# A hybrid decoder layer on one core: ten quads of seven products instead of nine in eleven column pairs, bias loaded for four heads at once

## The chip, the cores and the metric

The kernel runs on one core of one Trainium2 chip. The metric is the device time of one execution in microseconds. All values are float32 in and out. The core's engines are TensorE (PE in the profile, with PEld for the loading of weights), VectorE (DVE), ScalarE (ACT), GpSimd (POOL) and SyncE (SP), which only issues transfers here.

## The reference

One layer: an RMS norm, one input projection to eight parts of 2048 columns, block-sparse attention with a bias by relative position on four of them, a short causal convolution on the other four, an output projection and a second RMS norm. The sequence has 256 positions, the width is 4096, there are 16 heads of 128, and with a block of 256 every query sees only its own block, so the attention is plain causal attention.

```
u = rmsnorm(x, norm_gain)                      # x: 256 x 4096
proj = u @ w_in                                # 4096 x 16384
q, k, v, z_a, hc, b_gate, c_gate, z_c = split(proj, 8)
l = q @ k.T * 128**-0.5 + bias[bucket(qpos - kpos)], causal     # per head
attn = softmax(l) @ v * silu(z_a)
conv = b_gate * short_conv(c_gate * hc, conv_w) * silu(z_c)     # three taps
h = x + concat(attn, conv) @ w_out             # 4096 x 4096
out = rmsnorm(h, final_gain)
```

Nearly all of the work is the two products with w_in (256 MB) and w_out (64 MB), which are read once.

## The kernel before

**Products.** The weights are taken in 20 pairs of column blocks of 512 (16 pairs of w_in, 4 of w_out). Within a pair the 4096 rows are taken as 16 quads: a quad is two row blocks of 128 times two column blocks of 512, one transfer of 1 MB. With the two halves of the 256 positions, a quad is a 2 x 2 times 2 x 2 block product. It is made in one of two ways: with eight block products, or with seven (Winograd's form of Strassen's algorithm). `ORDERS` gives the order of a pair's quads and `SEVENS` those of them that are made with seven; both come from a pattern string, in which S stands for a quad of seven and P for one of eight. Here a capital S or the word seven means such a quad. Products are summed over the quads in eight PSUM banks.

**Precision.** Each float32 operand is split into a rounded high part and the rest (hi and lo, lines 592 and 594), and each block product is three matmuls of 128 x 128 by 128 x 512: high by high, low by high, high by low (lines 666, 667 and 669). The cast to hi runs on ACT, the difference lo on DVE. An S needs, beside the split of the four raw blocks, three sums of blocks (lines 574 and 575 on DVE) and their split. A first sum of two blocks is made in DRAM ahead of time by a copy (SP, line 509) and an accumulating transfer (POOL, line 510), for at most three quads ahead.

**Units and rings.** A P is one unit of eight products, an S two units: four products with the raw blocks, then three with the sums. `split(u + 2)` loads, sums and splits two units ahead of PE; hi and lo have three slots each, the raw blocks three tiles. The stationary operands, made from x or from the mixer's output, stay in SBUF for all pairs (tiles k0 to k15): four parts for a quad that is always P, seven or eight where it is ever S (`SIZES`). The eighth is needed where a quad is S in one pair and P in a later one, because an S needs a difference in place of part 0 (`g_at`, `BOTH`). `made_up` makes the additional parts of a quad between two pairs (`RAISE`).

**Closing of a pair.** The last S of a pair finishes four banks, which `early` takes out (line 376 on ACT, lines 377 to 379 on DVE). The other four are taken behind the last quad by `two_done` (line 389). The last two quads of every pair are P.

**Attention and convolution** are laid between the products by counts of products: `tasks_of(p)` counts from the last S of pair p, `heads_of(p)` from the opening of the pair. The scores of the four heads of a group (`turn`, `scores`) run in the last two quads of pairs 1, 3, 5 and 7, the probabilities (`probs`) there and in the first quad of the next pair, `values` and `mixed` at the end of pairs 2, 4, 6 and 8; the convolutions at the end of pairs 10, 12, 14 and in pair 16. `bias_load` loads the bias of one head with eight transfers from a DRAM table, called in `scores` for the head after the next one (lines 262 to 272, 290), so that behind each addition (line 289) eight transfers stand in SP's queue. The pools' planner (the tile framework) places the instructions of each engine's queue by their readiness under its own costs, with the order of the program as priority; so neighbours in a queue can change places.

Of the kernel before, what the change touches and what calls it, by code (L numbers as in the profile page):

```python
# [10 lines left out]
F32 = mybir.dt.float32  # L11
# [6 lines left out]
P = 128  # L18
# [21 lines left out]
        "9": "PSPSSPSSPSSPSSPP", "m": "PSPSSPSPSSPSPSSP", "e": "PSPSPSPSPSPSSPPP", "f": "PSPSSPSPSSPSSPPP"}  # L40
KIND = "01999999" "99999999" "099e"
# [23 lines left out]
SEVEN = (0, 2, 4, 6, 8, 10, 12, 14, 11)  # L65
# [17 lines left out]
def of(pattern):  # L83
    n = pattern.count("S")
    return in_order(pattern, SEVEN[:n], EIGHT + SEVEN[n:]), set(SEVEN[:n])
# [7 lines left out]
BOTH = {q for q in range(NQ) for a, b in ((0, N_PAIRS), (N_PAIRS, N_PAIRS + NDP)) for p in range(a, b)  # L93
        if q in SEVENS[p] and any(q not in SEVENS[x] for x in range(p, b))}
# [5 lines left out]
RAISE = {(1, 1): 4, (1, 3): 6, (1, 6): 0, (1, 8): 2, (1, 10): 11,  # L100
# [8 lines left out]
def hymba_layer(ctx: ExitStack, tc: tile.TileContext, xT, xres, gain, w, convw, wout,  # L109
# [61 lines left out]
    def x_load(q):  # L171
        xr = pool.tile([P, 2, S], F32, name="xr", tag="pt", bufs=4)
        nc.sync.dma_start(xr, xT[q].rearrange("p (k t) -> p k t", k=2))
        return xr

# [40 lines left out]
    def squares(n):  # L216
        p, t = divmod(n, 2)
        xq = pool.tile([P, 2, B], F32, name="xq", tag="qk"[t]).rearrange("p n c -> p (n c)")
        nc.sync.dma_start(xq, xres[p][:, t * 2 * B:(t + 1) * 2 * B])
        nc.scalar.activation(xq, xq, AF.Square, accum_out=sx[:, t, p:p + 1])  # L220
# [22 lines left out]
    def bias_rows():  # L243

        tab = pool.tile([BUCKETS + 1, H], F32, name="tab", tag="lg", bufs=2)
        nc.vector.memset(tab, MASKED)
        nc.sync.dma_start(tab[:BUCKETS], relb)
        oh = pool.tile([BUCKETS + 1, 384], F32, name="oh", tag="bt", bufs=2)
# [3 lines left out]
        row = pool.tile([H, 384], F32, name="row", tag="lg", bufs=2)  # L252
# [9 lines left out]
    def bias_load(h):  # L262
        if h >= H:
            return
        bt = BT[h] = pool.tile([P, 384], F32, name="bt", bufs=2)

        base = bias_d.offset + h * COPIES * 384
        for a in range(0, P, COPIES):
            for c0, c1, at in ((0, S, P - 1), (S, 384, S - 1)):
                nc.sync.dma_start(bt[a:a + COPIES, c0:c1],  # L270
                                  bass.AP(tensor=bias_d.tensor, offset=base + at - a,
                                          ap=[[383, COPIES], [1, c1 - c0]]))
# [10 lines left out]
    def scores(h, n):  # L283
        qk, bt = QK.pop(h), BT.pop(h)
        ps = bank(n)
        nc.tensor.matmul(ps[:, :S], qk[:, P:S], qk[:, S:], start=True, stop=True)  # L286
        nc.tensor.matmul(ps[:, S:384], qk[:, :P], qk[:, S:384], start=True, stop=True)
        lg = pool.tile([P, 384], F32, name="lg", bufs=2)
        nc.vector.tensor_tensor(lg, ps[:, :384], bt, ALU.add)
        bias_load(h + 2)  # L290
        st = pool.tile([P, 6], F32, name="st", bufs=5)
        for i, (a, b) in enumerate(((0, S), (S, 384))):
            nc.vector.tensor_reduce(st[:, i:i + 1], lg[:, a:b], axis=AX.X, op=ALU.max, negate=True)
            nc.scalar.activation(lg[:, a:b], lg[:, a:b], AF.Exp, bias=st[:, i:i + 1],  # L294
                                 accum_out=st[:, 2 + i:3 + i])
        nc.vector.reciprocal(st[:, 4:6], st[:, 2:4])
        SM[h] = lg, st

    def probs(h, n):
        ps = bank(n)  # L300
        lg, st = SM[h]
        for j in range(3):
            nc.tensor.transpose(ps[:, j * P:(j + 1) * P], lg[:, j * P:(j + 1) * P], ident)  # L303
        PT[h] = pool.tile([P, 2 * S], F32, name="pt", bufs=4)[:, :384]
        nc.scalar.copy(PT[h], ps[:, :384])
# [206 lines left out]
    def load(n):  # L512
# [5 lines left out]
        if p == 0:  # L518
            if i == 0:
                nc.scalar.dma_start(g_sb, gain)  # L520
                xr = xrs[q] = pool.tile([P, 2, S], F32, name="xr", tag="pt", bufs=4)
                nc.scalar.dma_start(xr[:, 1], xT[q][:, S:])
            else:
                xrs[q] = x_load(q)
# [147 lines left out]
    for u, (n, kind, at, products) in enumerate(units):  # L672
# [36 lines left out]
        if p == 1 and i in (0, 4, 5):  # L709
            if i:  # L710
                bias_load(i - 4)
            else:
                bias_store(row)
# [22 lines left out]
        if (p, i + 1) in RAISE:  # L736
            q = RAISE[p, i + 1]
            raised[q] = x_load(q) if p < N_PAIRS else m_load(q)
        if (p, i) in RAISE:
            q = RAISE[p, i]  # L740
            made_up(q, x_scaled(q, raised.pop(q)) if p < N_PAIRS else raised.pop(q))
# [87 lines left out]
```

## Time and profile before

| what | value |
|---|---|
| time, median of 3 runs | 1698.26 us (1697.95 to 1698.77) |
| span of the profiled execution | 1696.2 us |
| PE, DVE, ACT busy | 99%, 90%, 62% of the span |
| granted TensorE clock | 0.998 |
| matmuls of the products | three lines, 2370 records each under their main operands |
| transfers | 452 MB, mean 267 GB/s |

The profile gives one execution, whose own time is the span of 1696.2 us from the first to the last instruction; the timed runs include what lies around it. Records are named by line, engine and operation and by the tiles out<-in. A matmul's record overlaps that of the next one. "Idle before" is an engine's idle time ahead of an instruction, with what ended it.

### The profile page before, as it was taken

Reading aid. Unit: us, or ns where it says so; the run is one execution under the profiler, and the core shown is the slowest. Engines: PE = TensorE matmul, PEld = TensorE weight load, DVE = VectorE, ACT = ScalarE, POOL = GpSimd, SP = SyncE. Lnnn points to the kernel's source line nnn. Section 1 sums busy time; section 2 is a strip of 40 time slices with the busy share of each in tenths; the row PEclk is TensorE's granted clock in tenths of the full one; section 3 lists DMA queues with packets and bytes.
Section 4 is the critical chain, followed back from the end, with each engine's and each line's share of the span. In section 5 each row is a group of like instructions: output and inputs, shape, how many; then the busy total and the mean of one; then the engine's idle time right before and its main releaser. Section 6 shows DMA issues by size and latency. Waiting matters only on the chain.

```text
span 1696.2 us, 20730 instructions
## 1 busy us (share of the span) xinstructions
PE 1682.2 (99%) x7562; PEld 1388.8 (82%) x7562; DVE 1527.7 (90%) x1307; ACT 1056.1 (62%) x1167; POOL 128.8 (8%) x162
## 2 busy tenths in 40 slices
PE   9999999999999999999999999999999999999997
PEld 7888888888888888888888888888888888878886
DVE  7989889888988898898998989899999999989887
ACT  6856755675667565755566565656565755656553
POOL 0000000000000000000000000000001000101000
PEclk9999999999999999999999999999999999999999
DMA  8878878778887878787888888888888889989884
GB/s 337 292 243 281 241 249 283 265 240 260 267 261 244 276 246 276 235 264 257 263 274 268 269 265 278 270 252 272 272 273 258 293 281 300 286 267 268 293 281 168
DMA packets 116625, 452.36 MB, mean 267 GB/s; under 512 B 16459, under 2 KB 21356, under 8 KB 93292
## 3 DMA queue, kind: packets, MB, share of 16 engines
q1 hardware_dynamic: 93772, 409.99, 67.2%
q0 software_dynamic: 22464, 40.90, 15.3%
q8 instruction: 59, 0.97, 0.2%
q14 instruction: 42, 0.34, 0.1%
q10 hardware_dynamic: 288, 0.15, 0.0%
HBM read 441.81 MB, written 90.96 MB: 314 GB/s over the span
## 4 chain that ended last, share of the span: by engine, by line
PE 98%; ACT 1%; issue 0%; DMA 0%; DVE 0%; DVEq 0%; SPq 0%; ACTq 0%
PE p L666 32%; PE p L667 32%; PE p L669 32%; PE p L279 0%; PE p L303 0%; ACT hi L592 0%; PE p L286 0%; DMA xr<-in_xT_dram 0%; ACT L294 0%; ACT L399 0%; PE p L312 0%; PE p L314 0%; PE p L313 0%; PE p L338 0%; PE p L358 0%
## 5 line engine op out<-in xcount | busy, mean ns | idle before, releaser
L666 PE MATMUL p<-hi,k 128*128 128x512 f32 x2370 | 921.8, 390 | 1.4 <-ACT hi L592 0.9
L667 PE MATMUL p<-hi,k 128*128 128x512 f32 x2370 | 922.5, 390 | 0.0
L592 ACT CAST hi<-raw 128x1024 fp32r<-128x1024 f32 (+1 forms) x638 | 636.5, 1044 | 302.5 <-PE p L667 224.2
L594 DVE TENSOR_TENSOR lo<-raw,hi 128x2048 fp32r<-128x2048 f32 (+1 forms) x323 | 723.5, 2247 | 70.6 <-ACT hi L592 70.3
L669 PE MATMUL p<-lo,k 128*128 128x512 f32 x2370 | 637.3, 392 | 0.0
L666 PEld LDWEIGHTS p<-hi,k 128*128 128x128 f32 x2370 | 445.0, 188 | 94.9 <-ACT hi L592 1.3
L667 PEld LDWEIGHTS p<-hi,k 128*128 128x128 f32 x2370 | 444.8, 188 | 93.3 <-issue 0.6
L669 PEld LDWEIGHTS p<-lo,k 128*128 128x128 f32 x2370 | 442.6, 188 | 89.1 <-DVE lo L594 0.3
L592 ACT CAST hi<-sum 128x1536 fp32r<-128x1536 f32 x156 | 231.2, 1482 | 207.6 <-DVE sum L575 111.5
L594 DVE TENSOR_TENSOR lo<-sum,hi 128x1536 fp32r<-128x1536 f32 x156 | 273.5, 1753 | 28.2 <-ACT hi L592 26.6
L510 POOL DMA_DIRECT2D t<-in_w_dram x126 | 103.6, 822 | 1205.4 <-DMA t<-in_w_dram 958.0
L575 DVE TENSOR_TENSOR sum<-raw,sum 128x1024 f32<-128x1024 f32 x156 | 190.7, 1222 | 3.3
L574 DVE TENSOR_TENSOR sum<-raw 128x512 f32<-128x512 f32 x156 | 106.9, 685 | 9.0 <-DMA raw<-in_w_dram 8.3
L385 ACT ACTIVATE es<-es,rT 128x512 f32<-128x512 f32 x56 | 38.9, 719 | 15.5 <-DVE es L379 8.6
L510 POOL DMA_DIRECT2D t<-in_wout_dram x30 | 24.6, 820 | 298.4 <-DMA t<-in_wout_dram 259.6
L377 DVE TENSOR_TENSOR es<-p,es 128x512 f32<-128x512 f32 x20 | 13.8, 690 | 25.9 <-PE p L669 23.8
L592 ACT CAST hi<-hg 128x1536 fp32r<-128x1536 f32 x10 | 14.8, 1480 | 24.2 <-DVE hg L575 19.6
L376 ACT COPY es<-p 128x512 f32<-128x512 f32 x20 | 11.7, 583 | 26.8 <-PE p L669 26.8
L168 ACT CAST k<-c 128x512 fp32r<-128x512 f32 (+4 forms) x38 | 21.7, 598 | 8.0 <-DVE c L165 4.8
L169 DVE TENSOR_TENSOR k<-c,k 128x512 fp32r<-128x512 f32 (+4 forms) x38 | 24.3, 661 | 2.4 <-ACT k L168 2.4
L379 DVE TENSOR_TENSOR es<-p,es 128x1024 f32<-128x1024 f32 x20 | 24.4, 1218 | 0.1
L165 DVE TENSOR_TENSOR c<-c 128x128 f32<-128x128 f32 x72 | 17.7, 285 | 0.1
(112 smaller groups left out, 528.3 us busy)
## 6 DMA issues: line engine op xcount, KB each, us to landing
raw<-in_w_dram SPq DMA_DIRECT2D x128, 1024.0 KB, 6.3
raw<-in_w_dram SPq DMA_DIRECT2D x126, 768.0 KB, 6.2
raw<-t SPq DMA_DIRECT2D x156, 256.0 KB, 4.2
raw<-in_wout_dram SPq DMA_DIRECT2D x34, 1024.0 KB, 6.5
t<-in_w_dram SPq DMA_DIRECT2D x126, 256.0 KB, 6.3
t<-in_w_dram POOLq DMA_DIRECT2D x126, 256.0 KB, 5.9
raw<-in_wout_dram SPq DMA_DIRECT2D x30, 768.0 KB, 6.7
t<-in_wout_dram SPq DMA_DIRECT2D x30, 256.0 KB, 6.8
```

Of the source, the lines that this page charges most:

```text
L168: nc.scalar.copy(dst[:, :, 0], c)
L169: nc.vector.tensor_tensor(dst[:, :, 1], c, dst[:, :, 0].bitcast(F32), ALU.subtract)
L379: nc.vector.tensor_tensor(es[:, 1::2], acc[5][:, None, :].to_broadcast([P, 2, B]), es[:, 1:3], ALU.subtract)
L385: nc.scalar.activation(e, e, AF.Copy, scale=r)
L510: nc.gpsimd.dma_start(by_rows(t1), rest[:, :B], accum_op=ALU.add)
L574: nc.vector.tensor_tensor(t[:, 0], raw[:, 0], raw[:, 2], ALU.subtract)
L575: nc.vector.tensor_tensor(t[:, 1:], raw[:, 1::2], t[:, :1].to_broadcast([P, 2, B]), ALU.subtract)
L592: nc.scalar.copy(hi[:, b:b + half], src[:, b:b + half])
L594: nc.vector.tensor_tensor(lo[:, c], src[:, c], hi[:, c].bitcast(F32), ALU.subtract)
L666: nc.tensor.matmul(acc[b_], a, h_, start=s0, stop=False)
L667: nc.tensor.matmul(acc[b_], b, h_, start=False, stop=False)
L669: nc.tensor.matmul(acc[b_], a, l_, start=False, stop=s1)
```

## The change

Pairs 2 to 10, 12 and 14 take a new pattern t with ten S in place of nine: quad 9 is made with seven there. Pairs 11, 13, 15, 17 and 18 keep nine. Because quad 9 is S in some pairs and P in later ones, its operand tile has eight parts, and pair 1 makes the extra four behind its thirteenth quad. To make room in SBUF, the operands of quads 14 and 11 in the output pairs get seven parts instead of eight, and pair 19, where both are P, makes part 0 again from DRAM (`BACK`); the bias of a group of four heads is one tile, loaded by eight transfers at places 4 to 11 of pairs 1, 2, 4 and 6, and the logits are made in place in it; tiles of x, of the squares and of the bias table take the space of others (tags q, k, es, pt). A raised x quad is loaded right into the tile in which it is scaled. The reciprocals of the sums of exponentials move from `scores` to `probs`.

```
-KIND = "01999999" "99999999" "099e"
+        "t": "PSSPSSSPSSPSSSPP"}
+KIND = "01tttttt" "ttt9t9t9" "099e"
...
-SEVEN = (0, 2, 4, 6, 8, 10, 12, 14, 11)
+SEVEN = (0, 2, 4, 6, 8, 10, 12, 14, 11, 9)
...
+BOTH = {q for q in range(NQ) for p in range(N_PAIRS)
+        if q in SEVENS[p] and any(q not in SEVENS[x] for x in range(p, N_PAIRS))}
+LAST = N_PAIRS + NDP - 1
+BACK = dict(zip(((LAST, 2), (LAST, 6)), (q for q in ORDERS[LAST] if q in SEVENS[LAST - 1] - SEVENS[LAST] - BOTH)))
...
-RAISE = {(1, 1): 4, (1, 3): 6, (1, 6): 0, (1, 8): 2, (1, 10): 11,
+RAISE = {(1, 1): 4, (1, 3): 6, (1, 6): 0, (1, 8): 2, (1, 10): 11, (1, 12): 9,
...
+    def x_again(q):
+        c = ep.tile([P, 8, P], F32, name="c", bufs=2)
+        nc.sync.dma_start(c[:, :4], xT[q].rearrange("p (a b) -> p a b", a=4))
+        return c
+
+    def scale_again(q, c):
+        for j in range(2):
+            x = c[:, 2 * j:2 * j + 2]
+            nc.scalar.activation(x, x, AF.Copy, scale=g_sb[:, 2 * q + j:2 * q + j + 1])
+        return c
...
+    def bias_load(g, n):
+        if n == 0:
+            BT[g] = pool.tile([P, HG, 384], F32, name="bt")
+        a, (c0, c1, at) = n // 2 * COPIES, ((0, S, P - 1), (S, 384, S - 1))[n % 2]
+        nc.sync.dma_start(BT[g][a:a + COPIES, :, c0:c1],
+                          bass.AP(tensor=bias_d.tensor,
+                                  offset=bias_d.offset + g * HG * COPIES * 384 + at - a,
+                                  ap=[[383, COPIES], [COPIES * 384, HG], [1, c1 - c0]]))
...
-        lg = pool.tile([P, 384], F32, name="lg", bufs=2)
-        nc.vector.tensor_tensor(lg, ps[:, :384], bt, ALU.add)
-        bias_load(h + 2)
+        nc.vector.tensor_tensor(lg, ps[:, :384], lg, ALU.add)
...
-        nc.vector.reciprocal(st[:, 4:6], st[:, 2:4])
         SM[h] = lg, st
...
     def probs(h, n):
         ps = bank(n)
         lg, st = SM[h]
+        nc.vector.reciprocal(st[:, 4:6], st[:, 2:4])
...
+        if p in (1, 2, 4, 6) and 4 <= i < 12:
+            bias_load(p // 2, i - 4)
...
+        if (p, i + 1) in BACK:
+            raised[BACK[p, i + 1]] = m_load(BACK[p, i + 1])
+        if (p, i) in BACK:
+            parts(A[BACK[p, i]][:, :1], raised.pop(BACK[p, i])[:, :1])
```

More of the change, by code (lines that the diff above doesn't have):

```diff
@@ L83, in of @@
 def of(pattern):
-    n = pattern.count("S")
-    return in_order(pattern, SEVEN[:n], EIGHT + SEVEN[n:]), set(SEVEN[:n])
+    seven = SEVEN[:pattern.count("S")]
+    eight = dict.fromkeys(EIGHT + SEVEN[len(seven):])
+    return in_order(pattern, seven, [q for q in eight if q not in seven]), set(seven)
 ORDERS, SEVENS = zip(*([(FIRST0, {8, 10, 12, 14}), (SECOND, {4, 6, 8, 10, 12, 14})]
@@ L91 @@
                        + [(FIRST, {8, 6, 10, 12, 14})] + [of(PATS[k]) for k in KIND[N_PAIRS + 1:]]))
-BOTH = {q for q in range(NQ) for a, b in ((0, N_PAIRS), (N_PAIRS, N_PAIRS + NDP)) for p in range(a, b)
-        if q in SEVENS[p] and any(q not in SEVENS[x] for x in range(p, b))}
+BOTH = {q for q in range(NQ) for p in range(N_PAIRS)
+        if q in SEVENS[p] and any(q not in SEVENS[x] for x in range(p, N_PAIRS))}
+LAST = N_PAIRS + NDP - 1
+BACK = dict(zip(((LAST, 2), (LAST, 6)), (q for q in ORDERS[LAST] if q in SEVENS[LAST - 1] - SEVENS[LAST] - BOTH)))
+assert set(BACK.values()) | BOTH >= {q for p in range(N_PAIRS, LAST) for q in SEVENS[p] - SEVENS[LAST]}
+assert all(q in SEVENS[x] for q in BACK.values() for x in range(N_PAIRS + 1, LAST))
 SIZES = [8 if q in BOTH else 7 if any(q in x for x in SEVENS) else 4 for q in range(NQ)]
@@ L169, in parts, with x_tile, x_load @@
         nc.vector.tensor_tensor(dst[:, :, 1], c, dst[:, :, 0].bitcast(F32), ALU.subtract)
-    def x_load(q):
-        xr = pool.tile([P, 2, S], F32, name="xr", tag="pt", bufs=4)
+    def x_tile(i):
+        if i % 2 == 0:
+            cur["xr"] = pool.tile([P, 2, 2, S], F32, name="xr", tag="qk"[i // 2 % 2])
+        return cur["xr"][:, i % 2]
+    def x_load(i, q):
+        xr = x_tile(i)
         nc.sync.dma_start(xr, xT[q].rearrange("p (k t) -> p k t", k=2))
         return xr
+    def x_again(q):
[7 more added lines that the diff above has]
+        return c
     def x_scaled(q, xr):
@@ L217, in squares @@
         p, t = divmod(n, 2)
-        xq = pool.tile([P, 2, B], F32, name="xq", tag="qk"[t]).rearrange("p n c -> p (n c)")
+        if n == 0:
+            cur["xq"] = ep.tile([P, 4, B], F32, name="es")
+        xq = cur["xq"][:, 2 * t:2 * t + 2].rearrange("p n c -> p (n c)")
         nc.sync.dma_start(xq, xres[p][:, t * 2 * B:(t + 1) * 2 * B])
@@ L243, in bias_rows @@
     def bias_rows():
[L245 removed]
+        tab = pool.tile([BUCKETS + 1, H], F32, name="tab", tag="pt", bufs=4)
         nc.vector.memset(tab, MASKED)
         nc.sync.dma_start(tab[:BUCKETS], relb)
[L248 removed]
+        oh = pool.tile([BUCKETS + 1, 384], F32, name="oh", tag="pt", bufs=4)
         nc.sync.dma_start(oh, onehot)
@@ L251, in bias_rows @@
         nc.tensor.matmul(ps[:H, :384], tab, oh, start=True, stop=True)
-        row = pool.tile([H, 384], F32, name="row", tag="lg", bufs=2)
+        row = pool.tile([H, 384], F32, name="row", tag="pt", bufs=4)
         nc.vector.tensor_copy(row, ps[:H, :384])
@@ L260, in hymba_layer @@
     V, Z, Q, K, QK, SM, PT, AM, BT, MT = [{} for _ in range(10)]
[L262 to L272, printed above, removed]
+    def bias_load(g, n):
+        if n == 0:
+            BT[g] = pool.tile([P, HG, 384], F32, name="bt")
[4 more added lines that the diff above has]
+                                  ap=[[383, COPIES], [COPIES * 384, HG], [1, c1 - c0]]))
     def turn(h, n):
@@ L301, in probs @@
         lg, st = SM[h]
+        nc.vector.reciprocal(st[:, 4:6], st[:, 2:4])
         for j in range(3):
             nc.tensor.transpose(ps[:, j * P:(j + 1) * P], lg[:, j * P:(j + 1) * P], ident)
-        PT[h] = pool.tile([P, 2 * S], F32, name="pt", bufs=4)[:, :384]
+        PT[h] = pool.tile([P, 384], F32, name="pt", bufs=4)
         nc.scalar.copy(PT[h], ps[:, :384])
@@ L520, in load @@
                 nc.scalar.dma_start(g_sb, gain)
-                xr = xrs[q] = pool.tile([P, 2, S], F32, name="xr", tag="pt", bufs=4)
+                xr = xrs[q] = x_tile(i)
                 nc.scalar.dma_start(xr[:, 1], xT[q][:, S:])
             else:
-                xrs[q] = x_load(q)
+                xrs[q] = x_load(i, q)
         if n < LEAD:
@@ L708, in hymba_layer @@
                 token_scale()
[L709 to L713, printed above, removed]
+        if (p, i) == (1, 0):
+            bias_store(row)
+        if p in (1, 2, 4, 6) and 4 <= i < 12:
+            bias_load(p // 2, i - 4)
         if i == last_seven[p]:
```

8 lines of the change are left out of this document (4 added, 4 removed).

## The prediction, made before the change was run

> **What bounds the kernel now.** I read the first and fifth parts of the page first: who is busy, and with what.
>
> ```profile
> span 1696.2 us, 20730 instructions
> PE 1682.2 (99%) x7562; PEld 1388.8 (82%) x7562; DVE 1527.7 (90%) x1307; ACT 1056.1 (62%) x1167; POOL 128.8 (8%) x162
> ...
> L666 PE MATMUL p<-hi,k 128*128 128x512 f32 x2370 | 921.8, 390 | 1.4 <-ACT hi L592 0.9
> ...
> L592 ACT CAST hi<-sum 128x1536 fp32r<-128x1536 f32 x156 | 231.2, 1482 | 207.6 <-DVE sum L575 111.5
> L594 DVE TENSOR_TENSOR lo<-sum,hi 128x1536 fp32r<-128x1536 f32 x156 | 273.5, 1753 | 28.2 <-ACT hi L592 26.6
> ...
> L575 DVE TENSOR_TENSOR sum<-raw,sum 128x1024 f32<-128x1024 f32 x156 | 190.7, 1222 | 3.3
> L574 DVE TENSOR_TENSOR sum<-raw 128x512 f32<-128x512 f32 x156 | 106.9, 685 | 9.0 <-DMA raw<-in_w_dram 8.3
> ```
>
> TensorE (PE) is busy for 99% of the span and waits 1.4 us in all at its main line. But a matmul record lasts 390 ns and overlaps the next, so busy time does not give the pace. The chain of waits does. Here it is at the opening of pair 10, where each row of eight closes one quad of eight products:
>
> ```profile
> 860.99 1.81 PE p L669 x8
> 866.43 1.81 PE p L669 x8
> 876.63 1.81 PE p L669 x8
> 891.59 1.81 PE p L669 x8
> ```
>
> Two eights in a row lie 5.44 us apart: 24 matmuls of 0.227 us. From 866.43 to 876.63 there is one seven and one eight, 10.20 us, so a seven takes 4.76. From 876.63 to 891.59 two sevens and an eight take 14.96 = 5.44 + 2 x 4.76. PE runs at one pace without holes, and **a quad that goes from eight products to seven saves 0.68 us** (three matmuls), if PE stays the bound.
>
> Whether it does is a question for VectorE (DVE). The view of busy time by stretches answers it, cut where ScalarE (ACT) takes the first finished sum of a pair (line 376), so that a stretch holds the last two quads of one pair and the first fourteen of the next. Columns: stretch, its length, then PE, PEld, DVE, ACT and POOL busy, the granted clock, the share of the DMA engines, GB/s.
>
> ```profile
> 79.30:161.80 82.50, 82.50 (x364) 68.04 (x363) 74.91 (x89) 53.60 (x69) 2.62 (x3) 1.00 0.77 252
> 161.80:249.70 87.90, 87.90 (x406) 72.87 (x405) 77.10 (x67) 58.16 (x72) 7.41 (x9) 1.00 0.85 263
> 249.70:333.60 83.90, 83.90 (x388) 69.57 (x387) 75.45 (x59) 51.31 (x53) 7.37 (x9) 1.00 0.81 261
> ...
> 764.80:850.00 85.20, 85.20 (x393) 70.80 (x393) 76.32 (x60) 50.66 (x52) 7.38 (x9) 1.00 0.84 259
> 850.00:930.90 80.90, 80.90 (x359) 66.98 (x358) 73.59 (x52) 50.66 (x50) 7.39 (x9) 1.00 0.85 275
> 930.90:1013.70 82.80, 82.80 (x374) 68.55 (x373) 77.64 (x64) 49.87 (x51) 7.38 (x9) 1.00 0.85 264
> ...
> 1258.40:1340.80 82.40, 82.40 (x373) 68.22 (x372) 80.12 (x73) 52.52 (x57) 7.38 (x9) 1.00 0.84 267
> ...
> 1432.30:1507.20 74.90, 74.90 (x332) 62.00 (x331) 71.55 (x53) 42.67 (x42) 7.38 (x9) 1.00 0.90 282
> 1507.20:1589.50 82.30, 81.43 (x359) 66.87 (x359) 76.23 (x54) 49.23 (x50) 7.39 (x9) 1.00 0.84 269
> 1589.50:1666.30 76.80, 76.80 (x340) 63.62 (x339) 68.13 (x49) 46.34 (x46) 3.28 (x4) 1.00 0.76 267
> ```
>
> PE fills every stretch here but the one from 1507.20 on. DVE has 10.8 us free in pair 2's stretch (161.80), 8.45 in pair 3's, 8.9 in pair 9's and 7.3 in pair 10's (850.00). Pair 15's stretch is the measure of how far this can go: DVE 80.12 of 82.40, 97.2%, and PE still full. What DVE's free time consists of:
>
> ```profile
> DVE lo L594 <- ACT hi L592: 96.9, 119, 4.0
> DVE es L377 <- PE p L669: 23.8, 10, 4.3
> DVE sum L574 <- DMA raw<-in_w_dram: 8.3, 8, 1.9
> DVE st L296 <- ACT lg L294: 7.5, 8, 1.2
> ...
> ACT hi L592 <- PE p L667: 307.6, 241, 5.1
> ```
>
> Most of it is the wait for a cast, and the cast waits for PE to give back a slot of the three-deep ring (last row): DVE waits because it is ahead, so this time can be used.
>
> **The change part by part.** The pattern t has ten S (sevens) where 9 has nine, in pairs 2 to 10, 12 and 14: eleven quads lose three matmuls each. PE: 11 x 0.68 = **7.48 us less**.
>
> *DVE.* An eight needs one L594 of 128x2048; a seven needs that one too, and 0.685 + 1.222 + 1.753 = 3.66 us more. A t stretch is 0.68 shorter as well, so DVE's free time falls by 4.34: to 6.5 in pair 2's stretch, 4.1 in pair 3's, 4.6 in pair 9's and 3.0 in pair 10's, the tightest of those quoted: 77.25 of 80.22, 96.3%, still under the 97.2% of pair 15. The conv tasks of pairs 10, 12 and 14 run in the stretches of 11, 13 and 15 (77.64 of 82.80 and 80.12 of 82.40), and those three pairs keep nine sevens. So on average PE stays the bound everywhere.
>
> *Three sevens in a row*, which t has twice, are new; 9 has two at most. A seven takes DVE 5.95 us against PE's 4.76, an eight 2.29 against 5.44. Three sevens thus cost at most 3 x 1.19 = 3.6 us of lead, 1.2 more than two do. The records overlap a little (in pair 10's stretch DVE's groups sum to more than its busy time), so this is the upper end. The lead is seen behind the two sevens that close pair 17:
>
> ```profile
> 1503.58 1.76 DVE L594 TENSOR_TENSOR lo<-sum,hi 128x1536 fp32r<-128x1536 f32 x1
> ```
> ```profile
> 1508.84 0.84 PE L669 MATMUL p<-lo,k 128*128 128x512 f32 x3
> ```
>
> The low half is ready at 1505.34 and first used at 1508.84: 3.5 us early. With a third seven 2.3 remain. The smallest lead that I found where t brings sevens forward is at the opening of pair 2, behind the attention work of pair 1:
>
> ```profile
> 195.08 1.81 PE p L669 x8
> ```
> ```profile
> 190.04 4.49 DVE L594 TENSOR_TENSOR lo<-raw,hi 128x2048 fp32r<-128x2048 f32 x2 [1.21 <-ACT hi L592]
> ```
>
> The first of these two low halves, of the eight at place 2, is ready about 192.3 and used at 195.08, 2.8 us later. In t that place holds a seven, whose low products start after 8 matmuls instead of 16, 1.8 us earlier: 1.0 us of lead. DVE waits 1.21 us for ACT just before, so the two extra sums (1.91 us) partly fit into that hole. I take no stall; the bounds are 0 and 1.0 us in each of pairs 2, 4, 6 and 8.
>
> *ACT* gets one cast of 1.48 us per t stretch, at 50.66 of 80.90: no bound.
>
> *Transfers.* The rows of the queues (packets, MB, share of 16 engines):
>
> ```profile
> q1 hardware_dynamic: 93772, 409.99, 67.2%
> q0 software_dynamic: 22464, 40.90, 15.3%
> ```
>
> q1 spends 67.2% of 1696.2 us on 410 MB, 2.78 us per MB on all 16 engines; q0 15.3% on 156 accumulates, 1.66 us each. An eight is 1.05 MB, 2.9 us. A seven adds the copy of a quarter (0.26 MB, 0.73 us) and the accumulate: 5.3 us. Nine and seven make 68.0 of 80.9 us (0.84; the row has 0.85); ten and six 70.6 of 80.2: 0.88. Pair 17's stretch ran at 0.90 with PE full. No time.
>
> *Pair 1* makes the extra parts of quad 9 behind its thirteenth quad, as it does for five quads now: a load, two scalings, four differences and two splits.
>
> ```profile
> L169 DVE TENSOR_TENSOR k<-c,k 128x512 fp32r<-128x512 f32 (+4 forms) x38 | 24.3, 661 | 2.4 <-ACT k L168 2.4
> ...
> L165 DVE TENSOR_TENSOR c<-c 128x128 f32<-128x128 f32 x72 | 17.7, 285 | 0.1
> ```
>
> On DVE 4 x 0.285 + 2 x 0.661 = 2.5 us, in a stretch where it is busy for 74.91 of 82.50. The load is the same as the five others have, but into the tile where it is scaled; SP issues it one quad ahead as theirs.
>
> *Bias.* 128 small transfers become 32 of four heads with the same bytes:
>
> ```profile
> L270 SPq DMA_DIRECT2D bt<-bias_d x128: 302/419/1150, 106.7 to 695.2; - x128
> DMA to landing us min/median/max: 1.6/2.4/5.0
> ```
>
> SP loses 96 issues of 0.42 us and the waits for the additions they hung on; the loads move to places 4 to 11 of pairs 1, 2, 4 and 6, one behind each quad's raw load. Behind them in SP's queue stand the next raw loads, but the tile's last readers (the transposes of the group before) are done in the pair's first quad, so the load doesn't wait. Even at four times 5.0 us it lands before the scores at the end of the pair. Nothing on the path.
>
> *Reciprocals* go to the probabilities: up to 7.5 us of DVE's waits (L296 above) fall away in pairs 2, 4, 6 and 8, just where the lead is shortest. *In the output pairs* quads 14 and 11 keep seven parts instead of eight, and pair 19 makes the overwritten one again: two loads, two 128x128 splits, beside DVE's 68.13 of 76.80 there. Nothing.
>
> **Sum:** 1696.2 - 7.48 = 1688.7 of span. The timed median of 1698.26 stands 2.1 above the profiled span, for what lies around it: 1690.8, and with the first crumbs of a stall **1690.9 us**, 0.43% faster.
>
> **The rivals.**
>
> *Small stalls (B).* DVE comes late at the opening of pairs 2, 4, 6 and 8, up to 1.0 us each, or at one or two closings: 2 to 6 us of the gain go, 1692.9 to 1697. For it: the short lead of pair 2. Against: the reciprocals' waits that leave the same place.
>
> *The closing of the pair (C), slower.* At the end of pair 17 ACT takes the finished sum first and casts the next quad only then:
>
> ```profile
> 1507.22 0.59 ACT L376 COPY es<-p 128x512 f32<-128x512 f32 x1 [3.68 <-PE p L669]
> ...
> 1508.07 1.28 ACT L637 ACT_TABLE_LOAD   x1
> ...
> 1509.47 5.77 ACT L592 CAST hi<-raw 128x1024 fp32r<-128x1024 f32 x6
> ```
> ```profile
> 1510.55 0.50 PE L666 MATMUL p<-hi,k 128*128 128x512 f32 x1 [0.87 <-ACT hi L592]
> ```
>
> The three matmuls from 1508.84 on were issued at 0.227 us each, so PE was ready at 1509.52 and loses 1.03 us. The order of copy and cast is chosen by the planner, and three sevens at the end of t make the cast later. In each of the eleven pairs this costs 11.3 us, 3.9 more than the gain: 1702.1. It turns the sign from 0.68 us per pair on. Against: in pair 17 a table load of 1.28 us stands between copy and cast, and PE is full in the stretches behind the other closings quoted.
>
> By the Trainium skill, "TensorE: Matmul & The Clock Gate", section "HAM oscillation", PE's clock halves only behind idle time of about 3.4 us. The trace agrees as far as it goes: the granted clock of the stretch with this hole is 1.00. By that page a hole three times as long would cost, as an estimate, some 1.7 us more each; the sum holds none.
>
> *Transfers (D), slower.* Three sevens ask for 15.9 us of transfers while PE takes 14.3. If nothing were prefetched, 1.6 us a run, two runs a pair, eleven pairs: 36 us, 1726. Against: three raw tiles, first sums made three quads ahead, and the eight behind each run gives back 2.5 us.
>
> *It doesn't do what it says (E):* DVE, not PE, sets the pace of t pairs, so the time stays at 1698. Against: 96.3% below the 97.2% seen.
>
> **How the numbers follow.** About 0.2% (3.4 us) is what a measurement of this kernel can tell from no change: faster below 1694.9, slower above 1701.7. Forecast 0.66 (1689.2 to 1692.8); B 0.18, two thirds of it still faster; C 0.10, of which 0.07 is past the bound; D 0.04; E 0.02. Faster 0.66 + 0.12 = 0.78; slower 0.07 + 0.04 = 0.11; same 0.06 + 0.03 + 0.02 = 0.11. The range takes the forecast and B, 0.84: 1689.2 to 1697.0.
>
> **What the profile after would show.** Right: L666 with 11 records fewer (2359); closings of quads 5.44 and 4.76 us apart as before; pair 10's stretch 80.2 us with DVE near 77; the wait of L594 for ACT down by a third or more; DMA share there 0.88. Wrong: idle time of PE before L666 or L669 released by ACT's cast or DVE's low half (at a pair's opening: B; right behind the copy of the finished sum: C; behind raw transfers: D), or t stretches that are not shorter (E).

## The result: slower by 0.6%, and the profile after

| | before | after |
|---|---|---|
| time, median of 5 runs | 1698.44 us (1697.95 to 1699.13) | 1708.5 us (1707.3 to 1708.95) |
| span of the profiled execution | 1696.2 us | 1705.5 us |
| ratio after : before | | 1.0058, 95% interval 1.0046 to 1.0071 |

The prediction was 1690.9 us, faster, with a range up to 1697.0. The kernel came out slower than before, past the bound of 0.2%. The first and fifth parts of the page of after, with the columns as before:

```profile
span 1705.5 us, 20704 instructions
PE 1680.9 (99%) x7529; PEld 1382.5 (81%) x7529; DVE 1562.0 (92%) x1348; ACT 1064.8 (62%) x1182; POOL 137.9 (8%) x173
...
L685 PE MATMUL p<-hi,k 128*128 128x512 f32 x2359 | 918.5, 391 | 5.5 <-DVE mt L385 3.8
```

The work is what was announced: 2359 records at the main line, 33 matmuls fewer over its three lines. PE's pace is the old one too. The chain of waits of after, at the opening of pair 10, closes three eights in a row at 5.44 us each:

```profile
861.78 1.81 PE p L688 x8
...
867.22 1.81 PE p L688 x8
...
872.66 1.81 PE p L688 x8
```

So 7.5 us of matmuls did go, and the span still grew by 9.3: some 16.8 us of holes came in. PE's share of 99% does not show them, but the difference of span and busy time does: 14.0 us before, 24.6 after (and part of a hole is covered by the tail of the record ahead of it). Where they lie, the busy time by stretches shows, cut at ACT's copy of the first finished sum of a pair, as before (stretch, length, PE, PEld, DVE, ACT, POOL, granted clock, share of the DMA engines, GB/s):

```profile
161.80:251.00 89.20, 88.04 (x404) 72.21 (x403) 81.36 (x75) 59.58 (x77) 8.23 (x10) 1.00 0.80 253
251.00:336.90 85.90, 84.84 (x387) 69.93 (x386) 77.33 (x61) 50.14 (x52) 8.19 (x10) 1.00 0.83 260
336.90:424.70 87.80, 86.96 (x399) 71.35 (x398) 79.99 (x69) 60.16 (x74) 8.20 (x10) 1.00 0.81 264
...
855.70:936.90 81.20, 81.20 (x359) 67.21 (x358) 75.86 (x54) 48.19 (x47) 8.20 (x10) 1.00 0.86 277
936.90:1021.70 84.80, 82.36 (x370) 67.56 (x369) 78.78 (x64) 51.29 (x52) 7.40 (x9) 1.00 0.83 265
...
1266.00:1350.10 84.10, 83.28 (x375) 68.67 (x375) 81.35 (x73) 52.88 (x56) 7.41 (x9) 1.00 0.84 265
```

At the closing of pair 1, at 161.8 us, both kernels stand at the same time. From there, with the lengths of the same view of both kernels; "lost" is the growth beyond what the change should give (-0.68 in the pairs that take t). ACT's copy is not a steady mark, though: the change itself moves it against PE, by up to 0.7 us. So the last column has what is lost when the cut lies on PE, where the low products that end the pair's last seven start (at pair 2: 250.63 before, 252.07 after):

| stretch from the closing of pair | before, us | after, us | lost, us | lost with the cut on PE, us |
|---|---|---|---|---|
| 1 | 87.9 | 89.2 | 2.0 | 2.1 |
| 2, 4, 6 | 83.9, 83.8, 83.9 | 85.9, 86.0, 86.0 | 2.7, 2.9, 2.8 | 1.9, 2.0, 1.9 |
| 3, 5, 7 | 88.1, 88.2, 87.2 | 87.8, 88.1, 86.9 | 0.4, 0.6, 0.4 | 1.2, 1.5, 1.0 |
| 8 | 85.2 | 84.0 | -0.5 | 0.0 |
| 9, 11, 13 | 80.9, 81.0, 80.9 | 81.2, 80.3, 80.2 | 1.0, 0.0, 0.0 | 0.2, 0.0, 0.0 |
| 10, 12, 14 | 82.8, 82.8, 82.4 | 84.8, 83.8, 84.1 | 2.0, 1.0, 1.7 | 2.8, 0.9, 1.1 |

By the last column some 12.7 of the 16.8 us stand in seven stretches and 3.7 in those from pairs 3, 5 and 7. All ten begin with closings at which other work runs: the scores at pairs 1, 3, 5 and 7, the values of the attention at 2, 4 and 6, the convolution at 10, 12 and 14. DVE is not full in those quoted (77.33 of 85.90, 78.78 of 84.80). The waits of PE, in us, their number and the longest:

```profile
PE p L685 <- DVE mt L385: 3.8, 3, 2.3
PE p L307 <- ACT qk L302: 2.8, 4, 1.0
PE p L331 <- DVE es L398: 2.7, 3, 0.9
PE p L685 <- ACT hi L611: 1.3, 1, 1.3
```

The main line waits 1.3 us for a cast; of the rest, the attention's and convolution's own instructions are one end or the other. To see what happens, here is ACT around the closing of pair 2, first before, then after (start, duration, instruction, idle time ahead of it and what ended it):

```profile
249.74 0.59 ACT L376 COPY es<-p 128x512 f32<-128x512 f32 x1 [4.59 <-PE p L669]
250.22 1.99 ACT L592 CAST hi<-raw 128x1024 fp32r<-128x1024 f32 x2
252.12 0.72 ACT L385 ACTIVATE es<-es,rQ 128x512 f32<-128x512 f32 x1
```
```profile
250.97 0.59 ACT L395 COPY es<-p 128x512 f32<-128x512 f32 x1 [3.82 <-PE p L688]
253.38 0.72 ACT L404 ACTIVATE es<-es,rQ 128x512 f32<-128x512 f32 x1 [1.83 <-DVE es L396]
254.01 1.98 ACT L611 CAST hi<-raw 128x1024 fp32r<-128x1024 f32 x2
```

In both, ACT waits for the finished sum (4.59 and 3.82 us) with the cast of the next quad, place 14, queued behind the copy. Before, the cast follows 0.48 us behind the copy's start. After, a scaling of an evacuated block (line 404) has come between; it waits 1.83 us for DVE, and the cast begins only 3.04 us behind the copy's start. PE meanwhile (the chain of waits of after, same place):

```profile
252.66 0.69 DVE es L396
253.35 0.28 DVE am L336
253.62 0.60 DVE es L397
254.22 0.19 DVE am L336
254.41 1.21 DVE es L398
255.62 0.14 issue
255.76 0.46 PE p L331 x2
256.22 0.23 PE p L685
```

For three microseconds the chain runs over DVE. Nine short matmuls of the attention (line 331 and its neighbours) now stand in PE's queue ahead of the first product of place 14 (three before), and they need the banks that DVE is just taking out (lines 396 to 398). PE has nothing else ahead of them and waits.

At the closing of pair 10 the queue of ACT shows the same turn, before and then after:

```profile
927.48 2.00 ACT L592 CAST hi<-raw 128x1024 fp32r<-128x1024 f32 x2 [0.79 <-PE p L667]
929.93 1.06 ACT L592 CAST hi<-raw 128x1024 fp32r<-128x1024 f32 x1 [0.45 <-PE p L667]
930.89 0.58 ACT L376 COPY es<-p 128x512 f32<-128x512 f32 x1
```
```profile
936.88 0.59 ACT L395 COPY es<-p 128x512 f32<-128x512 f32 x1 [4.11 <-PE p L688]
937.36 2.00 ACT L611 CAST hi<-raw 128x1024 fp32r<-128x1024 f32 x2
```

Before, place 14 is cast and part of place 15 too while PE still makes the last seven; after, ACT waits 4.11 us for that seven and only then casts. DVE gets its low half later by as much, while the convolution asks for it; 20 us on, PE waits 2.27 us:

```profile
957.26 0.50 PE L685 MATMUL p<-hi,k 128*128 128x512 f32 x1 [2.27 <-DVE mt L385]
```

Read from the order of the programs' queues, the cast of place 14 stands behind the copy of the finished sum in pairs 2, 4, 6, 17 and 18 before, and in pairs 2 to 7, 10, 12, 14, 15, 17 and 18 after. In PE's queue 9 short matmuls stand ahead of place 14 in pairs 2, 4 and 6 (before 3) and 7 in pairs 3, 5, 7 and 10 (before none).

### The profile page after: what moved, and what is told of

It is laid out like the page before. It is cut to its first block, busy times and chain, and to the rows that moved or that the text cites. A ratio compares the mean times of both kernels' runs of the same rounds, so it can differ in the third digit from the quotient of the medians.

```text
span 1705.5 us, 20704 instructions
## 1 busy us (share of the span) xinstructions
PE 1680.9 (99%) x7529; PEld 1382.5 (81%) x7529; DVE 1562.0 (92%) x1348; ACT 1064.8 (62%) x1182; POOL 137.9 (8%) x173
## 4 chain that ended last, share of the span: by engine, by line
PE 92%; DVE 4%; ACT 2%; issue 1%; DMA 1%; SPq 0%; DVEq 0%; ACTq 0%
PE p L685 30%; PE p L686 30%; PE p L688 30%; DVE lo L613 1%; DMA raw<-in_w_dram 1%; ACT hi L611 1%; DVE y L383 0%; ACT bt L313 0%; DVE es L397 0%; ACT L313 0%; DVE es L396 0%; DVE es L398 0%; PE p L307 0%; PE p L322 0%; PE p L331 0%
## 5 line engine op out<-in xcount | busy, mean ns | idle before, releaser
L611 ACT CAST hi<-sum 128x1536 fp32r<-128x1536 f32 x167 | 247.5, 1482 | 279.6 <-DVE sum L594 211.6
L613 DVE TENSOR_TENSOR lo<-sum,hi 128x1536 fp32r<-128x1536 f32 x167 | 292.8, 1753 | 16.6 <-ACT hi L611 15.0
L529 POOL DMA_DIRECT2D t<-in_w_dram x137 | 112.6, 822 | 1208.3 <-DMA t<-in_w_dram 880.3
L594 DVE TENSOR_TENSOR sum<-raw,sum 128x1024 f32<-128x1024 f32 x167 | 204.2, 1223 | 3.4
L593 DVE TENSOR_TENSOR sum<-raw 128x512 f32<-128x512 f32 x167 | 114.5, 686 | 0.6 <-DMA raw<-in_wout_dram 0.4
L396 DVE TENSOR_TENSOR es<-p,es 128x512 f32<-128x512 f32 x20 | 13.8, 691 | 41.6 <-PE p L688 31.9
L529 POOL DMA_DIRECT2D t<-in_wout_dram x30 | 24.6, 821 | 293.9 <-DMA t<-in_wout_dram 227.7
L175 DVE TENSOR_TENSOR k<-c,k 128x128 fp32r<-128x128 f32 (+3 forms) x42 | 25.5, 627 | 3.4 <-ACT k L174 3.4
L174 ACT CAST k<-c 128x128 fp32r<-128x128 f32 (+3 forms) x42 | 22.9, 567 | 3.5 <-DVE c L171 3.5
```

What stands on the lines that cost most here:

```text
L174: nc.scalar.copy(dst[:, :, 0], c)
L175: nc.vector.tensor_tensor(dst[:, :, 1], c, dst[:, :, 0].bitcast(F32), ALU.subtract)
L529: nc.gpsimd.dma_start(by_rows(t1), rest[:, :B], accum_op=ALU.add)
L593: nc.vector.tensor_tensor(t[:, 0], raw[:, 0], raw[:, 2], ALU.subtract)
L594: nc.vector.tensor_tensor(t[:, 1:], raw[:, 1::2], t[:, :1].to_broadcast([P, 2, B]), ALU.subtract)
L611: nc.scalar.copy(hi[:, b:b + half], src[:, b:b + half])
```

## The experiments

The readings at the start of the experiments, as the expectations name them: theory 1 is the order at the closing (copy and evacuation ahead of the split of place 14), rival C of the prediction; against it stood the three sevens in a row (DVE's lead) and the other parts of the change (bias, reciprocals). Within theory 1, 1a puts the price on the short matmuls that went ahead in PE's queue, 1b on the late cast itself. Each kernel is compared with the kernel before; "span" is that of its profiled execution. No kernel leaves out any of the computation.

**The cast ahead of the copy.** An ordering edge puts the copy of the finished sum behind the last cast that the program has issued by then, that of place 14.

```
-        nc.scalar.copy(es[:, 0], acc[1])
+        with tc.issue_after(cur["cast"].ins):
+            nc.scalar.copy(es[:, 0], acc[1])
...
-                nc.scalar.copy(hi[:, b:b + half], src[:, b:b + half])
+                cur["cast"] = nc.scalar.copy(hi[:, b:b + half], src[:, b:b + half])
```

> The changed kernel with one edge in ACT's queue: at each closing the copy of the first finished sum (es) stands behind the cast of the quad after the last seven (place 14). Nothing else is edited; TensorE's order follows from it: no attention or convolution matmul stands ahead of place 14 any more (in the changed kernel 7 to 9 do in pairs 2 to 7 and 7 in pair 10). Theory 1, the planner's order at the closings made TensorE's holes: 8 to 14 of the 17 us of holes go, 1692 to 1700 us, and pair 2's, 4's and 6's closings lose their 2.8 us each. Theory 2, DVE has no lead left in t pairs and the order is only a symptom: the holes move to L685 or L688 behind DVE's low halves, 1705 to 1709 us.

Measured: 1696.14 us, ratio 0.9986 (0.9977 to 0.9995), span 1694.7. One edge takes 12.4 us off the changed kernel. The stretches from the closings of pairs 2, 4 and 6 are 84.0 us (86.0 in after), those of 10, 12 and 14 83.1, 82.8 and 83.1 (84.8, 83.8 and 84.1); that of pair 1 keeps its 89.2. Of PE's waits those at line 331 are gone:

```profile
PE p L307 <- ACT qk L302: 3.6, 4, 1.0
...
PE p L686 <- DVE es L399: 1.0, 1, 1.0
PE p L686 <- DVE mt L385: 0.9, 1, 0.9
```

So the order at the closing is the cause of the slowdown. But the gain of 7.5 us is not there: this kernel is 2.3 us faster than before, and the edge has a value of its own (the last experiment). With the cut on PE the closings of pairs 2, 4 and 6 now lose 0.1 to 0.2 us, those of 12 and 14 nothing and that of 10 1.2; those of 1, 3, 5 and 7 still lose 0.9 to 1.8. The wait in pair 16 (line 399) is not the edge's own: a kernel below that has no edge in that pair keeps 0.8 us of it.

**The same bias, reciprocals and output parts, with nine sevens.**

```
-KIND = "01tttttt" "ttt9t9t9" "099e"
+KIND = "01999999" "99999999" "099e"
...
-RAISE = {(1, 1): 4, (1, 3): 6, (1, 6): 0, (1, 8): 2, (1, 10): 11, (1, 12): 9,
+RAISE = {(1, 1): 4, (1, 3): 6, (1, 6): 0, (1, 8): 2, (1, 10): 11,
```

> The changed kernel with nine sevens in every pair again (pattern 9 throughout, quad 9 not raised): what is left is the bias of four heads as one tile, the moved reciprocals, the other places in SBUF and the parts made again in pair 19. Theory 1 (the tenth seven changes the planner's order): 1696 to 1699 us, the closings of pairs 2, 4 and 6 in the order cast, copy. Theory 3 (the moved bias transfers or reciprocals cost the time): 1702 us or more.

Measured: 1698.92 us, 1.0001 (0.9991 to 1.0011), span 1697.1. The other parts of the change cost nothing that can be measured. In pairs 2 to 15 the cast of place 14 stands ahead of the copy everywhere, also in pairs 2, 4 and 6, where the kernel before has it behind. There it makes no difference: with the cut on PE these closings are within 0.2 us of those before.

**Two sevens at the closing instead of three.** The same ten quads, with the run of three moved from the end to the start of the pair.

```
-        "t": "PSSPSSSPSSPSSSPP"}
+        "t": "PSSSPSSSPSSPSSPP"}
```

> The changed kernel with the ten sevens of t laid as PSSSPSSSPSSPSSPP: the pair closes on two sevens as in pattern 9, three in a row only at its opening. Three sevens at the closing as the cause: the holes behind them go, 1693 to 1700 us. Theory 1: the planner's order at the closings is the same as in the changed kernel (copy ahead of cast in pairs 2 to 7, 10, 12, 14, 15), so is the time, 1705 to 1710 us.

Measured: 1702.55 us, 1.0022 (1.0012 to 1.0033), span 1701.7: neither interval. The copy stands ahead of the cast in the same pairs as in after, so that three sevens at the end are not what turns the order. Yet it is 6 us less. Two things besides the pattern differ: 4 to 5 short matmuls stand ahead of place 14 in PE's queue in place of 7 to 9, and in pairs 2, 4 and 6 the cast begins 0.48 us behind the copy's start in place of 3.04. Which of them makes the same order cheaper, this run doesn't tell.

**Ten sevens in the convolution pairs alone** (10, 12 and 14).

```
-KIND = "01tttttt" "ttt9t9t9" "099e"
+KIND = "01999999" "99t9t9t9" "099e"
```

> The changed kernel with ten sevens in pairs 10, 12 and 14 alone (nine elsewhere). Here the planner keeps the cast ahead of the copy in pairs 2 to 14; only pair 15's copy goes ahead. Theory 1: 3 x 0.68 = 2.0 us are gained and up to 1 us lost at each of three closings: 1695 to 1698.5 us. Theory 2 (DVE has no lead in t pairs): the stretches of pairs 11, 13 and 15 lose 4.7 us as in the changed kernel, 1699 to 1703 us.

Measured: 1698.07 us, 0.9996 (0.9987 to 1.0005), span 1696.4: theory 1's interval. With t in these three pairs the order turns in pair 15 alone, and not at their own closings, where it did turn in after. In after it did not turn in pairs 8 and 9, which lie among pairs of t. So neither the pattern of a pair nor that of its neighbours decides it.

Line 307 waits here too (2.0 us in two places), as it does not in the kernel with nine sevens throughout. The places are the closings of pairs 1 and 7, and the pairs on both sides of them have no tenth seven:

```profile
180.35 0.70 PE L307 MATMUL p<-qk 128*128 128x256 f32 x2 [1.02 <-ACT qk L302]
```

With the cut on PE, the stretch from the closing of pair 1 takes 89.0 us here and 88.7 in after, against 87.1 with nine sevens throughout. Up to there the last and this kernel differ only in quad 9's eight parts, of which pair 1 makes four. ACT makes their two casts (line 174, 0.71 us) just behind the closing and starts the copy that line 307 waits for at 179.73, against 177.04 without them. So what the closing of pair 1 loses comes with these parts, not with the tenth seven of pair 2.

**PE's order alone.** The cast stays late; the short matmuls are issued behind the last high product of the unit in which they are called, so that none stands ahead of place 14.

```
-            nc.tensor.matmul(acc[b_], b, h_, start=False, stop=False)
+            cur["h"] = nc.tensor.matmul(acc[b_], b, h_, start=False, stop=False)
...
-                        f(*args)
+                        with tc.issue_after(cur["h"].ins):
+                            f(*args)
```

> The changed kernel with edges in TensorE's queue alone: an attention or convolution task stands behind the high matmuls that the program has issued before it, so that none is ahead of place 14 (7 to 9 are in the changed kernel). ACT's copy still stands ahead of the cast of place 14 in pairs 2 to 10, 12 and 15. Theory 1a, the tasks ahead of place 14 wait for DVE's evacuation and are the price: the 8.4 us at the closings of pairs 2, 4, 6 and about 2 at pair 10's go, 1697 to 1701 us. Theory 1b, the late cast is the price: the hole moves to L685 behind ACT's cast, about 1 us in each of twelve closings, 1704 to 1709 us.

Measured: 1708.14 us, 1.0061 (1.0044 to 1.0078), span 1706.2. The order of copy and cast is not quite that of after: it has turned in pairs 8 and 9 too, and not in 14. Nothing is gained; 1a falls. The holes moved to the main line (waits of PE; then ACT at the closing of pair 2):

```profile
PE p L685 <- ACT hi L611: 8.2, 5, 2.1
```
```profile
250.75 0.59 ACT L395 COPY es<-p 128x512 f32<-128x512 f32 x1 [3.83 <-PE p L688]
252.68 0.72 ACT L404 ACTIVATE es<-es,rQ 128x512 f32<-128x512 f32 x1 [1.34 <-DVE es L396]
253.31 1.98 ACT L611 CAST hi<-raw 128x1024 fp32r<-128x1024 f32 x2
```

Without the short matmuls PE reaches place 14 and finds its cast only begun. In after they covered that wait; it stood behind them.

**The kernel before, with the cast made late.** In pairs 2 to 7, 10, 12, 14 and 15 the split of place 14 is issued behind the copy, as in after.

```
-        nc.scalar.copy(es[:, 0], acc[1])
+        cur["copy"] = nc.scalar.copy(es[:, 0], acc[1])
...
-        if u + 2 < len(units) and not early_now:
+        late_cast = p in (2, 3, 4, 5, 6, 7, 10, 12, 14, 15) and i == last_seven[p] and not end_of_quad
+        if u + 2 < len(units) and not early_now and not late_cast:
...
+            if p in (2, 3, 4, 5, 6, 7, 10, 12, 14, 15):
+                with tc.issue_after(cur["copy"].ins):
+                    split(u + 1)
```

> The kernel before with nine sevens, and only ACT's order changed: in pairs 2 to 8, 10, 12, 14 and 15 the cast of place 14 stands behind the copy of the finished sum. TensorE's order keeps its 3 tasks ahead of place 14 in pairs 2, 4 and 6 and has none elsewhere. Theory 1b: eight closings more at the 1.03 us of pair 17, 1704 to 1710 us. Theory 1a: 1698 to 1702 us.

Measured: 1700.72 us, 1.0014 (1.0004 to 1.0023), span 1698.6. That is 1a's interval, though its reason fell in the run before. The cast of place 14 went late in pair 8 as well. This is 2.3 us more than the kernel before, which has the cast late in pairs 2, 4 and 6 already, and 4.1 more than the kernel of nine sevens with the cast first everywhere (the last experiment); it is not 16. What the late cast adds to PE's waits is at the convolutions, and small:

```profile
PE p L666 <- DVE mt L366: 2.1, 3, 0.7
```

At the attention's closings PE waits nowhere. With the cut on PE, the closings of pairs 10, 12 and 14 each lose 0.9 us here, and those of 12 and 14 in after 0.9 and 1.1: there the late cast costs the same with nine sevens as with ten. At 2, 4 and 6 it costs nothing here, and 1.8 us in after (1.9 or 2.0 less the 0.1 to 0.2 that stay with the cast first). So the late cast alone is not the price there; three short matmuls stand ahead of place 14 here, nine in after, and no scaling stands between copy and cast. That ten sevens leave DVE too little lead for a late split would be another reading. No run shows it, and the next two speak against it.

**The scaling behind the cast as well as behind the copy, then with PE's order too.** The first edit keeps the order copy, cast, and forbids only that the scaling comes between; the second adds the edges of the kernel with PE's order.

```
+        cur["first"] = cur["cast"]
...
-        nc.scalar.activation(e, e, AF.Copy, scale=r)
+        with tc.issue_after(cur["first"].ins):
+            nc.scalar.activation(e, e, AF.Copy, scale=r)
```

> The changed kernel with one edge in ACT's queue: at a closing the scalings of the evacuated sums stand behind the cast of place 14. In the changed kernel one scaling, which waits for DVE's first evacuation, stands between the copy and this cast in pairs 2, 4 and 6. The copy stays ahead of the cast in the same pairs, and TensorE keeps its 7 to 9 tasks ahead of place 14. If the scaling between them is the price in these pairs: 4 to 6 us less than the changed kernel, 1702.5 to 1704.5 us. If the copy ahead of the cast or the tasks are: 1707 to 1709 us.

> The same and the edges in TensorE's queue (no task ahead of place 14). With TensorE's edges alone the hole behind pairs 2, 4 and 6 was 2.25 us behind the cast. If it was the scaling: about 0.2 us there, and 6 us less in all than with those edges alone, 1700 to 1703.5 us. If it was the copy: 2 us holes stay, 1706 to 1709 us.

Measured: 1708.85 us, 1.006 (1.0045 to 1.0075), span 1705.4, and 1705.25 us, 1.004 (1.0026 to 1.0054), span 1703.5. The scaling alone is not the price: PE still has its nine matmuls ahead. With both, 2.9 us come back against PE's order alone, less than expected and in neither interval. The hole has moved once more, to the low half. DVE and PE at the closing of pair 2 in the second kernel:

```profile
251.98 0.69 DVE L397 TENSOR_TENSOR es<-p,es 128x512 f32<-128x512 f32 x1 [3.03 <-PE p L690]
252.78 0.69 DVE L398 TENSOR_TENSOR es<-p,es 128x512 f32<-128x512 f32 x1
253.50 1.22 DVE L399 TENSOR_TENSOR es<-p,es 128x1024 f32<-128x1024 f32 x1
254.65 2.28 DVE L615 TENSOR_TENSOR lo<-raw,hi 128x2048 fp32r<-128x2048 f32 x1
```
```profile
256.98 1.19 PE L690 MATMUL p<-lo,k 128*128 128x512 f32 x4 [0.70 <-DVE lo L615]
```

DVE waits 3.03 us for the last seven with nothing that it may do, then takes out three tiles (0.69, 0.69 and 1.22), then makes the low half for 2.28. Had the cast been made in its 3.03 idle microseconds, the low half would have been made there too. So it is the whole split of place 14, on both engines, that stands behind the closing; no one neighbor in a queue is the price.

It is not that DVE has fallen behind with ten sevens: this low half begins 3.2 us behind the start of the last seven's low products (251.49). With nine sevens and the late cast it begins no sooner, 3.4 us behind it (254.03 against 250.65), and PE doesn't wait, because it has short matmuls to do until then. In pairs 3, 5, 7 and 10 it does begin 2.1 us later than with nine sevens, but there it stands behind all three evacuations on DVE, with nine sevens behind one: order again. With the cast first, the low half of place 14 is ready 4.5 us ahead of its use in pairs 3, 5, 7, 10, 12 and 14, with ten sevens as with nine.

**What eats the gain when the cast is first.** Line 307 (the scores) waits 3.6 us for the copies of q and k in that kernel. Its ACT at the closing of pair 3:

```profile
348.08 1.28 ACT L313 ACT_TABLE_LOAD   x1
349.37 0.51 ACT L313 ACTIVATE bt<-bt,st 128x256 f32<-128x256 f32 x1
...
351.14 0.56 ACT L302 COPY qk<-p 128x512 f32<-128x512 f32 x1
```

The copy stands behind a table load of 1.28 us and the exponentials of two heads. Two kernels try to get it out of there; both keep the edge, but for pair 16. The first puts the scores of the later two heads at counts 15 and 16 rather than 13 and 15. The second takes the exponentials out of `scores` into a task of their own, behind the copies:

```
-            nc.scalar.activation(lg[:, a:b], lg[:, a:b], AF.Exp, bias=st[:, i:i + 1],
-                                 accum_out=st[:, 2 + i:3 + i])
...
+    def exps(h, n):
+        for x in (h, h + 1):
+            lg, st = SM[x]
+            for i, (a, b) in enumerate(((0, S), (S, 384))):
+                nc.scalar.activation(lg[:, a:b], lg[:, a:b], AF.Exp, bias=st[:, i:i + 1],
+                                     accum_out=st[:, 2 + i:3 + i])
...
-                                (9, turn, 2, 1), (11, probs, 0, 6), (12, turn, 3, 7), (13, scores, 2, 5),
-                                (14, probs, 1, 1), (15, scores, 3, 6)):
+                                (9, turn, 2, 1), (10, turn, 3, 6), (11, exps, 0, 0), (12, scores, 2, 7),
+                                (13, scores, 3, 5), (14, probs, 0, 1), (15, probs, 1, 6), (16, exps, 2, 0)):
```

> The kernel of the run with the cast first (1696.1 us), without its edge in pair 16, and with the scores of a group's third and fourth head two places and one place later (counts 15 and 16 in place of 13 and 15). If its remaining holes are what they look like, TensorE waiting 0.9 us in each of four closings for the copy of the third head's q and k, and 1.2 us behind pair 16: 1691.5 to 1694.5 us. If DVE or ACT is simply full there, the hole only moves to another matmul: 1695 to 1697 us.

Measured: 1695.93 us, 0.9985 (0.9976 to 0.9995), span 1694.3. A miss: the wait went from line 307 to line 322 with the same 3.6 us. The wait in pair 16 stays too, without the edge there:

```profile
PE p L322 <- ACT qk L302: 3.6, 4, 1.0
...
PE p L686 <- DVE es L399: 0.8, 1, 0.8
```

> The kernel with the cast first, without its edge in pair 16, and with the exponentials of a pair of heads behind the q and k copies of the next pair of heads in ACT's queue (turn of the third and fourth head at counts 9 and 10, the first two heads' exponentials at 11, scores 2 and 3 at 12 and 13, probabilities 0 and 1 at 14 and 15, exponentials 2 and 3 at 16). In the two runs before, TensorE waits 3.6 us in four closings for these copies, which stand behind a table load and eight exponentials. If the order is the cause: the 3.6 us go, 1691.5 to 1694 us. If ACT is simply late there: 1695 to 1697 us.

Measured: 1692.86 us, 0.9967 (0.9955 to 0.998), span 1691.0. The wait is gone; the longest at the main line is 0.9:

```profile
PE p L691 <- DVE mt L390: 0.9, 1, 0.9
PE p L691 <- ACT pt L329: 0.7, 3, 0.2
```

This version beats both kernels: by 0.33% the one before, by 15.6 us the one after.

**The same with two sevens at the closing.**

> The same with the sevens laid as PSSSPSSSPSSPSSPP, two at the closing. If DVE's lead behind three sevens still costs something with the order right: up to 3 us less than the run before. If only the order counted: equal within 1 us.

Measured: 1692.68 us, 0.9967 (0.9955 to 0.9979), span 1690.5, equal to the last. With the cast first, the place of the run of three sevens does not matter.

**The kernel before, with the cast first.** The edge of the first experiment on the kernel with nine sevens.

> The kernel before (nine sevens, old bias) with the edge that puts the copy behind the cast, in every pair. Only pair 17's hole of 1.03 us is behind this order there: 1696.5 to 1698.5 us. What the run with ten sevens and the cast first gains over this one is what the tenth seven is worth with the order right: 7.5 us less what DVE's lost lead costs.

Measured: 1696.6 us, 0.9989 (0.998 to 0.9998), span 1694.4. The edge alone is worth 1.8 us there. So ten sevens with the edge alone (span 1694.7) bring nothing over nine with it: the 7.5 us are all eaten by new holes. With the exponentials moved they bring 3.4 us (1691.0 against 1694.4). Whether moving them would help nine sevens wasn't tried; the waits of PE in that kernel hold no row for the matmul of line 307 (line 286 there).

## Why the prediction was wrong

*The matmuls: right.* 11 records fewer at each of three lines, at the old pace; 7.5 us of PE's work went, and the cast-first kernel with the exponentials moved shows a part of it in the span.

*DVE on average: right, and not the answer.* It said 77.25 of 80.22 in pair 10's stretch; 75.86 of 81.20 came. No stretch quoted is as full as pair 15's was (97.2%). The wait of the low half for the cast (waits of DVE, after) fell by a quarter, not a third:

```profile
DVE lo L613 <- ACT hi L611: 72.4, 78, 4.2
DVE es L396 <- PE p L688: 31.9, 13, 4.0
```

The second row is the one that it should have thought of: DVE waits 31.9 us at thirteen closings (23.8 at ten before) for the last seven. Free time on average is no free time at a closing, where the work that would fill it stands behind the very thing that is waited for. The lead was judged well: at the closing of pair 2 in after, the low half of the third seven is ready at 249.14 and used at 252.07, 2.9 us early, where the prediction left 2.3.

*"So on average PE stays the bound everywhere": the step that failed.* The sum has no term for the closings; it counted 0 for what turned out 16.8 us, nearly all of it at ten of them. Putting the cast first takes 10.8 us off the span of after and 1.8 off that of before, so about 9.0 of the 16.8 are the turned order. Rival C had the mechanism: ACT takes the finished sum ahead of the next quad's cast. It held 0.10. Three things in its weighing were wrong:
- Its counter-argument, that PE was full behind the other closings, was no evidence against the order. In pairs 2, 4 and 6 of the kernel before the copy already stood ahead of the cast (249.74 and 250.22). It cost nothing there, but with little to spare: the low half of place 14 of pair 2 was ready at 255.16 and used at 255.52. With nine sevens, turning the order at the other closings too cost 2.3 us. The question should have been what the order costs when more stands in the same queues.
- Its price was 1.03 us in each of eleven pairs. With the cut on PE, the edge takes back 1.8 us in each of pairs 2, 4 and 6, 1.6 in 10, 1.0 and 1.1 in 12 and 14, and 0.6 or less in 3, 5 and 7, though the order turned there too. The price goes with the tasks that share the closing: evacuations and attention on DVE, the scaling on ACT, short matmuls that wait for banks on PE.
- Its reason, three sevens at the end of t, was not it. With two at the end the order turned in the same pairs. Three make the same order dearer by 6 us, and with the cast first the pattern makes no difference.

*The opening of pairs 2, 4, 6 and 8 (rival B): not seen.* Taken at 0, with up to 1.0 as the bound. None of PE's waits in after at a raw quad's low half reaches the list; the losses begin with the closings.

*Transfers and bias: right at nothing.* The share came to 0.86 in pair 10's stretch (0.88 predicted); with nine sevens, the new bias, reciprocals and output parts measured 1.0001.

*Pair 1's added parts: a second term wrongly put at nothing.* The prediction weighed them by DVE's free time in the stretch ahead of the closing. They cost at the closing behind them: 1.9 us (89.0 against 87.1) between two kernels that both have nine sevens there, 1.0 of it as the visible wait at line 307.

*The reciprocals' move* was taken as a help to DVE. A part that was not priced at all is the copies of q and k on ACT, which stand behind the exponentials at four closings: 2.8 us in after, 3.6 with the cast first, and 3.3 us of span when the exponentials are moved (1691.0 against 1694.3, with the same edges). The copies stood behind exponentials before too: at pair 1's closing the third head's begins at 177.33 in the kernel before, behind a table load at 174.27, and PE doesn't wait. What is new is that ACT comes to them later. At pair 1 quad 9's parts bring that; at 3, 5 and 7 it isn't shown what does, and the wait at pair 7 without a tenth seven near it says that it need not be one.

*The clock: right.* The longest wait of PE in the rows of after is 2.3 us, the granted clock 0.998 as before. The Trainium skill, "TensorE: Matmul & The Clock Gate", section "HAM oscillation", puts the halving of the clock behind about 3.4 us of idle time; these waits are shorter, and the trace agrees with it as far as it goes. Three times the hole of 1.03 us, for which the prediction works out a price, is 3.1 us and stays below it too.

What stays open: why the planner turns the order. Its costs were not looked into; shown is only that after has it turned against before in pairs 3, 5, 7, 10, 12, 14 and 15, and that with t in pairs 10, 12 and 14 alone it turns in pair 15 alone. Open in part are the other 4 us, those that still lie between the 7.5 us of matmuls and the 3.4 gained in the best kernel. The traces show where they are. Cut on PE and compared with nine sevens and the cast first, the best kernel loses 1.0 us at the closing of pair 1, 0.6 at each of 3, 5 and 7, and 1.1 at that of pair 10. The last is the 0.9 of waiting for line 390 and the part of it that the record ahead covers; what makes the others was not looked into.

## What to carry to other kernels

Where a planner orders the queues, a change in the amount of work can turn an order far from the edit. Before trusting a sum, list for each closing which instruction waits there for the last result, what is queued behind it on that engine, and whether that could have run in the wait; an explicit edge at such a place was worth 12.4 us here, more than the change itself. An engine's mean free time says nothing of that, and a hole filled at one place (the short matmuls, the scaling) opens behind the next instruction of the same late chain until the head of the chain, here the cast, is moved. To see where time is lost, cut the stretches on the engine that is the bound, not at an instruction that the change can move.
